# Cross-entropy with label smoothing: rows by blocks of 128, results turned on VectorE and stored in 128-byte pieces

## The chip, the cores and the metric

One core of one Trainium2 chip. The metric is device time in microseconds of one execution. The profile covers a little less: its span was about 1.8 us shorter than the time for the kernel before. Fast runs of one kernel in one set lay within 0.6% of their median (within 0.4% for the kernel before); the median of the same kernel differed by up to 0.6% between sets of runs (87.83 us in the first, 87.28 to 87.33 in the later ones), so kernels are compared only with the runs of the kernel before from the same set. A run over 1.5% above the fastest of the same kernel is called slow and left out of the ratios.

## The reference

```python
log_probs = logits - max(logits)                       # logits: 256 x 32000 f32
log_probs = log_probs - log(sum(exp(log_probs)))
smooth_targets = smoothing / 32000, plus 1 - smoothing at the label
return -sum(smooth_targets * log_probs, axis=-1)       # 256 f32
```

Per row the kernel needs the sum of exp(x), the sum of x and the logit at the label. 32.8 MB come in, 1 KB goes out.

## The kernel before

The 256 rows are two "blocks" of 128, one row per partition each. A block is streamed in tiles; each tile goes to VectorE (sum of x, L121) and to ScalarE (exp and its sum, L131). Large tiles share a ring of three buffers; the late, small tiles have buffers of their own. Tiles are named by their columns: the 6400 tile is the second of block 1. A transfer is "issued" when a queue sends it off, and it has "landed" when the last of its semaphore updates has come.

```python
WIDTHS = ((8000, 8000, 8000, 8000),
          (7872, 6400, 4736, 3584, 2752, 2176, 1728, 1472, 1280))
x = logits.rearrange("(p r) c -> p (r c)", r=R)        # partition p holds rows 2p, 2p+1
lab = small.tile([P, 2 * R], I32)                      # 128 pieces of 16 B, ScalarE's queue
...
for r in range(R):
    for t, w in enumerate(ws):
        xt = ring.tile(...) if w >= 6000 else tail.tile(...)
        nc.sync.dma_start(out=xt[:, :w], in_=x[:, col : col + w])   # SyncE's queue
        ...  # L121 on VectorE, L131 on ScalarE
    nc.scalar.activation(out=lse[:], in_=esum[:, n - 1 : n], func=AF.Ln, bias=se_pre[:])
    nc.vector.tensor_tensor(out=res[:, r : r + 1], in0=lse[:], in1=lin[:], op=ALU.add)
nc.sync.dma_start(out=out.rearrange("(p r) -> p r", r=R), in_=res[:])  # 128 pieces of 8 B
```

The softmax here doesn't subtract the row's maximum and nothing guards it: scores larger than these inputs give would overflow.

Of the kernel before, what the change touches and what calls it, by code (L numbers as in the profile page):

```python
# [7 lines left out]
FP32 = mybir.dt.float32  # L8
BF16 = mybir.dt.bfloat16
I32 = mybir.dt.int32  # L10
ALU = mybir.AluOpType
# [11 lines left out]
def _exp_ln_table(arch: str) -> int | None:  # L23
    try:
        tables = hw_specs.get_activation_tables(arch)
    except Exception:
        return None
    for i, (_, funcs) in enumerate(tables.items()):
        if {AF.Exp, AF.Ln, AF.Copy}.issubset(funcs):
            return i  # L30
    return None


@with_exitstack
def kernel(
    ctx: ExitStack,
    tc: tile.TileContext,
    logits: bass.AP,
    labels: bass.AP,
    smoothing: bass.AP,  # L40
    out: bass.AP,
):
    nc = tc.nc
    B, C = logits.shape
    P = nc.NUM_PARTITIONS
    R = B // P
    assert B == R * P and len(WIDTHS) == R
    assert all(sum(ws) == C for ws in WIDTHS)
    eps = float(smoothing)
    c_small = eps / float(C)  # L50
    c_big = 1.0 - eps

    ring = ctx.enter_context(tc.tile_pool(name="ring", bufs=3))
    tail = ctx.enter_context(tc.tile_pool(name="tail", bufs=1))
    junk = ctx.enter_context(tc.tile_pool(name="junk", bufs=1))
    small = ctx.enter_context(tc.tile_pool(name="small", bufs=1))

    tbl = _exp_ln_table(nc.m.arch)
    if tbl is not None:
        nc.scalar.add_instruction(  # L60
            mybir.InstLoadActFuncSet(
                name=nc.get_next_instruction_name(),
                act_func_set_id=tbl,
                ins=[],
                outs=[],
            )
        )


    x = logits.rearrange("(p r) c -> p (r c)", r=R)  # L70

    lab = small.tile([P, 2 * R], I32, name="lab", tag="lab")
    nc.scalar.dma_start(
        out=lab[:], in_=labels.bitcast(I32).rearrange("(p f) -> p f", p=P)
    )
    rowoff = small.tile([P, R], I32, name="rowoff", tag="rowoff")
    for r in range(R):
        nc.gpsimd.iota(  # L78
            out=rowoff[:, r : r + 1],
            pattern=[[0, 1]],  # L80
            base=r * C,
            channel_multiplier=R * C,
        )
    flat_idx = small.tile([P, R], I32, name="flat_idx", tag="flat_idx")
    nc.gpsimd.tensor_tensor(  # L85
        out=flat_idx[:],
        in0=rowoff[:],
        in1=lab[:].rearrange("p (r two) -> p r two", two=2)[:, :, 0:1],
        op=ALU.add,
    )  # L90
    gat = small.tile([P, R], FP32, name="gat", tag="gat")
    for r in range(R):
        nc.gpsimd.indirect_dma_start(  # L93
            out=gat[:, r : r + 1],
            out_offset=None,
            in_=logits[:],
            in_offset=bass.IndirectOffsetOnAxis(ap=flat_idx[:, r : r + 1], axis=1),
        )

    res = small.tile([P, R], FP32, name="res", tag="res")  # L100
    col = 0
    for r in range(R):
        ws = WIDTHS[r]
        n = len(ws)
        esum = small.tile([P, n], FP32, name=f"esum{r}", tag=f"esum{r}")
        xsum = small.tile([P, n], FP32, name=f"xsum{r}", tag=f"xsum{r}")
        se_pre = small.tile([P, 1], FP32, name=f"se_pre{r}", tag=f"se_pre{r}")
        sx_pre = small.tile([P, 1], FP32, name=f"sx_pre{r}", tag=f"sx_pre{r}")
        lin_pre = small.tile([P, 1], FP32, name=f"lin_pre{r}", tag=f"lin_pre{r}")
        lin = small.tile([P, 1], FP32, name=f"lin{r}", tag=f"lin{r}")  # L110
        lse = small.tile([P, 1], FP32, name=f"lse{r}", tag=f"lse{r}")
        for t, w in enumerate(ws):
            if w >= RING_MIN:
                xt = ring.tile([P, max(WIDTHS[0])], FP32, name="xt", tag="xt")
            else:
                xt = tail.tile([P, w], FP32, name=f"xl{t}", tag=f"xl{t}")
            nc.sync.dma_start(out=xt[:, :w], in_=x[:, col : col + w])  # L117
            col += w
            h = w // 2
            jd = junk.tile([P, max(WIDTHS[0]) // 2], FP32, name="jd", tag="jd")  # L120
            nc.vector.scalar_tensor_tensor(  # L121
                out=jd[:, :h],
                in0=xt[:, :h],
                scalar=1.0,
                in1=xt[:, h:w],
                op0=ALU.mult,
                op1=ALU.add,
                accum_out=xsum[:, t : t + 1],
            )
            ja = junk.tile([P, max(WIDTHS[0])], BF16, name="ja", tag="ja")  # L130
            nc.scalar.activation(  # L131
                out=ja[:, :w],
                in_=xt[:, :w],
                func=AF.Exp,
                accum_out=esum[:, t : t + 1],
            )
            if t == n - 2:

                nc.vector.tensor_reduce(  # L139
                    out=sx_pre[:], in_=xsum[:, : n - 1], axis=AX.X, op=ALU.add  # L140
                )
                nc.vector.tensor_scalar(  # L142
                    out=lin_pre[:],
                    in0=sx_pre[:],
                    scalar1=-c_small,
                    scalar2=None,
                    op0=ALU.mult,
                )
                nc.vector.scalar_tensor_tensor(  # L149
                    out=lin_pre[:],  # L150
                    in0=gat[:, r : r + 1],
                    scalar=-c_big,
                    in1=lin_pre[:],
                    op0=ALU.mult,
                    op1=ALU.add,
                )
                nc.vector.tensor_reduce(  # L157
                    out=se_pre[:], in_=esum[:, : n - 1], axis=AX.X, op=ALU.add
                )
        nc.vector.scalar_tensor_tensor(  # L160
            out=lin[:],
            in0=xsum[:, n - 1 : n],
            scalar=-c_small,
            in1=lin_pre[:],
            op0=ALU.mult,
            op1=ALU.add,
        )
        nc.scalar.activation(  # L168
            out=lse[:], in_=esum[:, n - 1 : n], func=AF.Ln, bias=se_pre[:]
        )  # L170
        nc.vector.tensor_tensor(  # L171
            out=res[:, r : r + 1], in0=lse[:], in1=lin[:], op=ALU.add
        )
    nc.sync.dma_start(out=out.rearrange("(p r) -> p r", r=R), in_=res[:])


# [33 lines left out]
```

## Time and profile before

| | kernel before |
|---|---|
| time, median | 87.76 us (87.5 to 87.98) |
| span of the profiled run | 85.7 us |
| logits, mean rate over the span | 382 GB/s |
| ScalarE busy | 69% |
| VectorE busy | 44% |
| last store, issue to landing | 2.9 us |

The shares of busy time mislead here: ScalarE is idle early and full late. The costliest groups of the page (busy us and mean ns of one, then the idle time just before and what ended it) say so:

```profile
L131 ACT ACTIVATE ja<-xt 128x8000 bf16<-128x8000 f32 (+2 forms) x6 | 39.8, 6630 | 21.5 <-DMA xt<-in_logits_dram 21.5
L131 ACT ACTIVATE ja<-xl 128x4736 bf16<-128x4736 f32 (+6 forms) x7 | 16.2, 2314 | 0.3
```

Before the six large tiles ScalarE waited 21.5 us for data, before the seven late ones 0.3 us. The loads set the pace first; at the end loads and ScalarE run in step, with no slack in either.

### The profile page before, as it was taken

The page shows a single profiled execution, that of the slowest core. Times are in us where ns is not written, and L with a number is a line of the kernel's source. Part 1 is how long each engine was busy: PE and PEld are TensorE (multiplying, and loading weights), DVE is VectorE, ACT ScalarE, POOL GpSimd, SP SyncE. Part 2 cuts the span into 40 slices and gives each one's busy share as a digit, 9 for nine tenths or more (in the row PEclk, how much of TensorE's full clock was granted, in tenths as well). Part 3 has the DMA queues.
Part 4 walks back from the last instruction along what each step waited for, and adds up shares of the span by engine and source line. Part 5 has one row for each costly group of instructions (what it writes and reads, how often), then busy time and mean ns, then how long its engine had stood idle before and what let it go on. Part 6 is the DMA issues. An engine that isn't in the chain of part 4 may idle for free.

```text
span 85.7 us, 167 instructions
## 1 busy us (share of the span) xinstructions
DVE 37.3 (44%) x38; ACT 59.1 (69%) x29; POOL 6.5 (8%) x9
## 2 busy tenths in 40 slices
DVE  0000009900495009920694029706909294566700
ACT  5000009992499709992599829996999999999900
POOL 1000008973000000000000000000000000000000
DMA  7699899997999989999899989989999999997000
GB/s 209 269 433 433 344 463 478 433 463 343 433 478 433 448 358 433 478 433 460 367 397 470 470 382 418 490 354 424 442 431 428 394 425 424 413 415 323 0 1 0
DMA packets 2224, 32.77 MB, mean 382 GB/s; under 512 B 560, under 2 KB 560, under 8 KB 944
## 3 DMA queue, kind: packets, MB, share of 16 engines
q1 hardware_dynamic: 2016, 32.77, 90.3%
q10 hardware_dynamic: 144, 0.00, 0.1%
q0 software_dynamic: 64, 0.00, 0.1%
HBM read 32.77 MB, written 0.00 MB: 382 GB/s over the span
## 4 chain that ended last, share of the span: by engine, by line
DMA 58%; ACT 34%; issue 2%; SPq 1%; DVE 0%; ACTq 0%
DMA xt<-in_logits_dram 58%; ACT ja L131 33%; SPq L117 1%; ACT lse L168 0%; DVE res L171 0%; ACTq L131 0%
## 5 line engine op out<-in xcount | busy, mean ns | idle before, releaser
L131 ACT ACTIVATE ja<-xt 128x8000 bf16<-128x8000 f32 (+2 forms) x6 | 39.8, 6630 | 21.5 <-DMA xt<-in_logits_dram 21.5
L121 DVE SCALAR_TENSOR_TENSOR jd<-xt 128x4000 f32<-128x4000 f32 (+2 forms) x6 | 25.1, 4175 | 31.0 <-DMA xt<-in_logits_dram 31.0
L131 ACT ACTIVATE ja<-xl 128x4736 bf16<-128x4736 f32 (+6 forms) x7 | 16.2, 2314 | 0.3
L121 DVE SCALAR_TENSOR_TENSOR jd<-xl 128x2368 f32<-128x2368 f32 (+6 forms) x7 | 10.3, 1476 | 7.7 <-DMA xl<-in_logits_dram 7.7
L85 POOL TENSOR_TENSOR flat_idx<-rowoff,lab 128x2 int32<-128x2 int32 x1 | 4.1, 4084 | 12.2 <-DMA lab<-in_labels_dram 12.2
L93 POOL DMA_INDIRECT gat<-in_logits_dram,flat_idx x2 | 2.1, 1028 | 0.6 <-issue 0.3
L171 DVE TENSOR_TENSOR res<-lse,lin 128x1 f32<-128x1 f32 x2 | 0.3, 160 | 3.5 <-ACT lse L168 3.5
L60 ACT ACT_TABLE_LOAD x1 | 1.3, 1283 | 0.7 <-PEq L191 0.7
L131 ACT ACTIVATION_READ_ACCUMULATOR ja<-xl 128x1 f32 x7 | 1.3, 186 | 0.0
L157 DVE TENSOR_REDUCE se_pre<-esum 128x1 f32<-128x3 f32 (+1 forms) x2 | 0.3, 158 | 2.1 <-ACT ja L131 2.1
L131 ACT ACTIVATION_READ_ACCUMULATOR ja<-xt 128x1 f32 x6 | 1.1, 186 | 0.0
L168 ACT ACTIVATE lse<-esum,se_pre 128x1 f32<-128x1 f32 x2 | 0.6, 294 | 0.1
L121 DVE DVE_READ_ACCUMULATOR jd<-xl 128x1 f32 x7 | 0.6, 82 | 0.0
L121 DVE DVE_READ_ACCUMULATOR jd<-xt 128x1 f32 x6 | 0.5, 82 | 0.0
L149 DVE SCALAR_TENSOR_TENSOR lin_pre<-gat,lin_pre 128x1 f32<-128x1 f32 x2 | 0.3, 159 | 0.1
L139 DVE TENSOR_REDUCE sx_pre<-xsum 128x1 f32<-128x3 f32 (+1 forms) x2 | 0.3, 158 | 0.1
L160 DVE SCALAR_TENSOR_TENSOR lin<-xsum,lin_pre 128x1 f32<-128x1 f32 x2 | 0.3, 158 | 0.1
L142 DVE TENSOR_SCALAR lin_pre<-sx_pre 128x1 f32<-128x1 f32 x2 | 0.3, 154 | 0.1
L78 POOL IOTA rowoff<- 128x1 int32 x2 | 0.2, 118 | 0.4 <-PEq L205 0.4
L191 POOL MEMSET const-uint8-127<- 128x1 uint8 x1 | 0.1, 118 | 0.0
L191 POOL MEMSET const-float32-0.0<- 128x1 f32 x1 | 0.1, 98 | 0.2 <-issue 0.2
L191 POOL MEMSET const-bfloat16-1.0<- 128x1 bf16 x1 | 0.1, 113 | 0.0
(1 smaller groups left out, 0.1 us busy)
## 6 DMA issues: line engine op xcount, KB each, us to landing
xt<-in_logits_dram SPq DMA_DIRECT2D x4, 4000.0 KB, 21.5
xt<-in_logits_dram SPq DMA_DIRECT2D x1, 3936.0 KB, 21.3
xt<-in_logits_dram SPq DMA_DIRECT2D x1, 3200.0 KB, 19.4
xl<-in_logits_dram SPq DMA_DIRECT2D x1, 2368.0 KB, 24.6
xl<-in_logits_dram SPq DMA_DIRECT2D x1, 1792.0 KB, 28.4
xl<-in_logits_dram SPq DMA_DIRECT2D x1, 1376.0 KB, 31.3
xl<-in_logits_dram SPq DMA_DIRECT2D x1, 1088.0 KB, 33.4
xl<-in_logits_dram SPq DMA_DIRECT2D x1, 864.0 KB, 35.0
```

Source lines behind the costliest of these rows:

```text
L60: nc.scalar.add_instruction(mybir.InstLoadActFuncSet(name=nc.get_next_instruction_name(), act_func_set_id=tbl, ins=[], outs=[],))
L85: nc.gpsimd.tensor_tensor(out=flat_idx[:], in0=rowoff[:], in1=lab[:].rearrange("p (r two) -> p r two", two=2)[:, :, 0:1], op=ALU.add,)
L93: nc.gpsimd.indirect_dma_start(out=gat[:, r : r + 1], out_offset=None, in_=logits[:], in_offset=bass.IndirectOffsetOnAxis(ap=flat_idx[:, r ...
L117: nc.sync.dma_start(out=xt[:, :w], in_=x[:, col : col + w])
L121: nc.vector.scalar_tensor_tensor(out=jd[:, :h], in0=xt[:, :h], scalar=1.0, in1=xt[:, h:w], op0=ALU.mult, op1=ALU.add, accum_out=xsum[:, t ...
L131: nc.scalar.activation(out=ja[:, :w], in_=xt[:, :w], func=AF.Exp, accum_out=esum[:, t : t + 1],)
L139: nc.vector.tensor_reduce(out=sx_pre[:], in_=xsum[:, : n - 1], axis=AX.X, op=ALU.add)
L142: nc.vector.tensor_scalar(out=lin_pre[:], in0=sx_pre[:], scalar1=-c_small, scalar2=None, op0=ALU.mult,)
L149: nc.vector.scalar_tensor_tensor(out=lin_pre[:], in0=gat[:, r : r + 1], scalar=-c_big, in1=lin_pre[:], op0=ALU.mult, op1=ALU.add,)
L157: nc.vector.tensor_reduce(out=se_pre[:], in_=esum[:, : n - 1], axis=AX.X, op=ALU.add)
L168: nc.scalar.activation(out=lse[:], in_=esum[:, n - 1 : n], func=AF.Ln, bias=se_pre[:])
L191: nc = _bacc.Bacc("TRN2", target_bir_lowering=False, num_devices=1)
```

## The change

Block r becomes rows 128r to 128r+127, so that a block's 128 results are one contiguous 512 B of the output. Each block's results, one column of a 128x32 tile, are turned by a 32x32 transpose per group of partitions; then partitions 0, 32, 64 and 96 hold 32 results each, and the store has four pieces of 128 B in place of 128 of 8 B. The diff, cut to its core:

```diff
-    x = logits.rearrange("(p r) c -> p (r c)", r=R)
-    lab = small.tile([P, 2 * R], I32, name="lab", tag="lab")
+    lab = small.tile([P, R, 2], I32, name="lab", tag="lab")
     nc.scalar.dma_start(
-        out=lab[:], in_=labels.bitcast(I32).rearrange("(p f) -> p f", p=P)
+        out=lab[:], in_=labels.bitcast(I32).rearrange("(r p two) -> p r two", r=R, two=2)
     )
 ...  # iota base and multiplier follow the rows
 ...  # SQ = 32; one 128x32 tile res[r] per block, set to 0 by GpSimd; col starts at 0 in each block
-            nc.sync.dma_start(out=xt[:, :w], in_=x[:, col : col + w])
+            nc.sync.dma_start(out=xt[:, :w], in_=logits[r * P : (r + 1) * P, col : col + w])
 ...  # inside the loop over blocks:
-            out=res[:, r : r + 1], in0=lse[:], in1=lin[:], op=ALU.add
-        )
-    nc.sync.dma_start(out=out.rearrange("(p r) -> p r", r=R), in_=res[:])
+            out=res[r][:, 0:1], in0=lse[:], in1=lin[:], op=ALU.add
+        )
+        rest = small.tile([P, SQ], FP32, name=f"rest{r}", tag=f"rest{r}")
+        nc.vector.transpose(out=rest[:], in_=res[r][:])
+        nc.sync.dma_start(
+            out=out[r * P : (r + 1) * P].rearrange("(g i) -> g i", i=SQ),
+            in_=rest[0:P:SQ, :],
+        )
```

More of the change, by code (lines that the diff above doesn't have):

```diff
@@ L80 @@
             pattern=[[0, 1]],
-            base=r * C,
-            channel_multiplier=R * C,
+            base=r * P * C,
+            channel_multiplier=C,
         )
@@ L87 @@
         in0=rowoff[:],
-        in1=lab[:].rearrange("p (r two) -> p r two", two=2)[:, :, 0:1],
+        in1=lab[:, :, 0:1],
         op=ALU.add,
@@ L98 @@
         )
-    res = small.tile([P, R], FP32, name="res", tag="res")
-    col = 0
+    SQ = 32
+    res = []
     for r in range(R):
+        t = small.tile([P, SQ], FP32, name=f"res{r}", tag=f"res{r}")
+        nc.gpsimd.memset(t[:], 0.0)
+        res.append(t)
+    for r in range(R):
+        col = 0
         ws = WIDTHS[r]
```

## The prediction

> **What bounds the kernel now.** I read the page's chain first, then the groups with their idle times, then the windows of DMA rate, then the timeline around 40 to 60 us, and last the tail.
>
> The chain that ended last:
>
> ```profile
> ## 4 chain that ended last, share of the span: by engine, by line
> DMA 58%; ACT 34%; issue 2%; SPq 1%; DVE 0%; ACTq 0%
> DMA xt<-in_logits_dram 58%; ACT ja L131 33%; SPq L117 1%; ACT lse L168 0%; DVE res L171 0%; ACTq L131 0%
> ```
>
> More than half of the span is the wait for logits, the rest mostly the exponential (L131). To see whether the loads ever pause, the windows (us, busy times, clock, DMA share, GB/s):
>
> ```profile
> 20.00:30.00 10.00, 4.33 (x2) 6.96 (x2) 0.00 (x0) 1.00 1.03 442
> 40.00:50.00 10.00, 4.65 (x4) 7.26 (x3) 0.00 (x0) 1.00 1.00 429
> 50.00:60.00 10.00, 5.68 (x3) 8.28 (x3) 0.00 (x0) 1.00 0.97 418
> 60.00:70.00 10.00, 6.20 (x5) 9.94 (x5) 0.00 (x0) 1.00 1.00 425
> 70.00:80.00 10.00, 5.99 (x14) 9.81 (x11) 0.00 (x0) 1.00 0.89 367
> ```
>
> They don't: from 12 to about 79 us the DMA engines are full at some 430 GB/s. From 60 us on ScalarE is full too. The shrinking widths have been tuned so that each late tile lands just as the exponential before it ends; the timeline shows this (start, length, engine, line; in brackets the idle time before):
>
> ```profile
> 50.92 6.76 ACT L131 ACTIVATE ja<-xt 128x7872 bf16<-128x7872 f32 x1 [2.00 <-DMA xt<-in_logits_dram]
> 58.58 5.54 ACT L131 ACTIVATE ja<-xt 128x6400 bf16<-128x6400 f32 x1 [0.81 <-DMA xt<-in_logits_dram]
> 64.24 2.63 DVE L121 SCALAR_TENSOR_TENSOR jd<-xl 128x2368 f32<-128x2368 f32 x1 [2.15 <-DMA xl<-in_logits_dram]
> 64.24 4.15 ACT L131 ACTIVATE ja<-xl 128x4736 bf16<-128x4736 f32 x1
> ...
> 78.39 1.43 ACT L131 ACTIVATE ja<-xl 128x1472 bf16<-128x1472 f32 x1
> 78.40 0.93 DVE L121 SCALAR_TENSOR_TENSOR jd<-xl 128x736 f32<-128x736 f32 x1 [0.74 <-DMA xl<-in_logits_dram]
> ```
>
> VectorE waits for the DMA and starts its tile in the same hundredths of a microsecond as ScalarE: data and ScalarE are ready together. So there is no slack in the loads after about 40 us: if they slip by d, the end slips by d, less a few hundredths. The tail:
>
> ```profile
> 81.34 0.29 ACT L168 ACTIVATE lse<-esum,se_pre 128x1 f32<-128x1 f32 x1
> 81.66 0.16 DVE L171 TENSOR_TENSOR res<-lse,lin 128x1 f32<-128x1 f32 x1 [0.63 <-ACT lse L168]
> 81.85 0.35 SPq L174 DMA_DIRECT2D out_dram<-res  x1
> ```
> ```profile
> out_dram<-res SPq DMA_DIRECT2D x1, 1.0 KB, 2.9
> ```
>
> The store is issued at 81.85, lands 2.9 us later (84.78), and 0.95 us of closing instructions bring the span to 85.7. The measured 87.5 to 88.0 is the span plus about 1.8 us.
>
> [...] the 1 KB store takes 2.9 us, though the last of its packets ended at about 82.9, so 1.9 us of it come after the data left; and the queue of SyncE stands still at its waits (23.3 us in all before the store of L174). [...] The old store has 128 packets of 8 B, the new one four of 128 B: [...] 32 times fewer. In the trace the semaphore updates of the old store's 16 engines come one after the other from 83.09 to 84.78, which looks like writes that queue up on one small stretch of memory. [...] No transpose is in this trace, so I price it by its neighbours. [...] Row starts go from 256,000 B to 128,000 B apart here; [...] the first ran at 430 GB/s, so I expect no change of rate.
>
> **The change, part by part.**
>
> Rows. Block r is now rows 128r to 128r+127 rather than every second row. Tile widths, sizes, packet lengths and the work on ScalarE and VectorE stay as they were: 0.
>
> Labels. Each partition's two labels now come from two places, so 256 pieces of 8 B instead of 128 of 16 B. The old label load took 12.3 us for 2 KB: its packets take turns with those of the first logits tile on every engine (both have 8 per engine, both landed at 13 us). With 16 per engine I expect it at about 22.5 us, with the second tile. That pushes flat_idx (4.1 us) and the two gathers (landed by 27.2) back by 9.5 us, to some 36.7. Their reader L149 ran at 36.90, and VectorE has nothing urgent until the next tile at 41.57. Hidden: 0. The two memsets on GpSimd lie in its 12.2 us idle: 0.
>
> First store. This is the part that I think matters most, and the diff doesn't show it. In the instruction order of the changed kernel, SyncE's queue holds: four loads of 8000, the load of 7872, the store of block 0, then the load of 6400 and all later ones. The store waits for the first transpose. Before, the 6400 load was issued at 39.13, as soon as ScalarE gave its buffer back, 11 us ahead of need. Now:
> - block 0's res starts at 48.95 and takes 0.16, so 49.11; transpose about 0.19 plus a 0.03 gap, so 49.33; store issued at 49.36, takes 0.35 on the queue, so 49.71; the 6400 load is issued at about 49.76.
> - Meanwhile the engines run out: the 7872 tile lands at 50.89, its last packets end between 49.7 and 50.4 on the 16 engines. First packets of the kernel's first load came 1.0 us after its issue (0.74 to 1.75), so the new ones start at about 50.8, and on a pipe that has to fill again.
> - Size of the hole: the first tile was issued at 0.74 and released ScalarE at 12.96; later tiles of that size come 9.54 us apart (12.96, 22.57, 32.15, 41.57). So a load on an empty pipe has 12.96 - 0.74 - 9.54 = 2.68 us over its streaming time. The 6400 tile streams in 9.54 x 0.8 = 7.63. Release at 49.76 + 2.68 + 7.63 = 60.07 instead of 58.52: 1.5 us late. The kernel's first load may have met start-up costs that don't return, and the spread of the engines is reset, so I take 1.4.
> - The loads behind it are issued about 0.45 us apart and their semaphore lanes are free soon enough (7872 landed at 50.89, the store of block 0 by about 52), so they follow without a second hole. All are 1.4 later, and so is the end: +1.4.
>
> Second transpose. It is on the tail's path: a VectorE instruction of one column takes 0.16, the 4000-column one of L121 4.33, so 1.04 ns a column; 32 columns make 0.19, with the hand-over 0.03: +0.22.
>
> Second store. Same 0.35 issue, then four packets on (I expect) four engines. The first engine of the old store reported 1.24 us after issue, the last 2.93. With no queue of small writes I expect 1.3 to 2.0, say 1.5: 2.93 - 1.5 = -1.4.
>
> Sum: +1.4 + 0.22 - 1.4 = +0.2. On 87.76 this makes 88.0.
>
> **The rivals.**
>
> The store in the queue is hidden anyway. For it: the engines still have 1 us of work when the load is issued at 49.76, and its tile is needed only at 58.5. Against: it is rate, not need, that sets the landing, and an engine idle for 1 us is never given back. The time would be 87.76 + 0.22 - 1.4 = 86.6, still within 2%.
>
> The small store costs its receipt whatever its shape. [...] Against: the spread of 1.7 us between the engines' updates. With no gain at all, 87.76 + 1.4 + 0.22 = 89.4, just inside 2%.
>
> The new row distance, or label packets that disturb two tiles rather than one, slow the loads. 1% of 78 us of loading is 0.8 us; nothing in the trace speaks for it but nothing excludes it. Together with the hole it would give 88.8 or more.
>
> The gathers come so late that VectorE stalls in order at L149. It would need 4.5 us more than I estimate before the tile at 41.57 is held up; then the buffer ring would slip too. Unlikely.
>
> **Range and chances.** The hole may be 0.9 to 1.7, the store's gain 0.6 to 1.6, the transpose is known to 0.1; the two large terms are independent and cancel. 8 times in 10 I expect 87.0 to 89.1. For faster by 2% (under 86.0) the hole would have to be absent and the store better than estimated: 0.05. For slower by 2% (over 89.5) the store would have to gain nothing, or the loads be slower: 0.08. Within 2%: 0.87.
>
> **What would show each step right or wrong.** The timeline should show SyncE's load of 6400 columns at about 49.8 instead of 39.1, right after an out store; the DMA row should dip in the slices near 51 us; ScalarE should wait some 2.2 us, not 0.81, before the 6400 tile, start it near 60.0 and then run without waits to the logarithm at about 82.8. The last transpose should take about 0.2, the last store land 1.3 to 2.0 after issue. The label load should land near 22 us and flat_idx start then, with no tile before 49 us moved. If the 6400 tile starts at 58.6 as before, the hole is wrong; if the last store still takes 2.9, the gain is; if the tiles before 49 us come at other than 9.5 us spacing, the row distance matters and I missed it.

The sum came to +0.2: +1.4 for the hole, +0.22 for the second transpose, -1.4 for the last store, all three estimated from the trace of the kernel before. That the new row distance changes no rate was the expectation from the 430 GB/s of the old one; experiment 4 tests it.

## The result, and the profile after

| | before | after |
|---|---|---|
| time, median of 4 | 87.83 us | 88.84 us |
| ratio, 95% interval | | 1.0116 (1.0079 to 1.0154) |
| same on another occasion, 11 and 5 runs | 87.30 us | 88.62 us, ratio 1.0146 (1.0123 to 1.0170) |

A ratio is the mean time of one kernel's fast runs over that of the other's of the same rounds, so not quite the ratio of the medians. The change costs 1.2 to 1.5%: within 2%, inside the predicted range, but +1.0 to +1.3 us where +0.2 was predicted.

SyncE's queue first, in the timeline of the kernel before and then of the changed one (start, time from the first to the end of the last of the group, line, count):

```profile
0.74 38.72 SPq L117 DMA_DIRECT2D xt<-in_logits_dram  x6
39.51 11.73 SPq L117 DMA_DIRECT2D xl<-in_logits_dram  x7
```
```profile
0.74 29.38 SPq L119 DMA_DIRECT2D xt<-in_logits_dram  x5
49.73 0.63 SPq L179 DMA_DIRECT2D out_dram<-rest  x1
50.45 0.34 SPq L119 DMA_DIRECT2D xt<-in_logits_dram  x1
50.85 3.53 SPq L119 DMA_DIRECT2D xl<-in_logits_dram  x7
```

Before, the sixth large load was out by 39.5 us and the late ones followed at once. After, five large loads were issued, then the queue stood until block 0's store, and the sixth large load went out at 50.45. The DMA engines' view of the same moment, in 2 us windows (busy times, clock, then DMA share and GB/s), before and after:

```profile
50.00:52.00 2.00, 1.08 (x1) 1.08 (x1) 0.00 (x0) 1.00 1.01 435
52.00:54.00 2.00, 2.00 (x1) 2.00 (x1) 0.00 (x0) 1.00 0.95 410
```
```profile
50.00:52.00 2.00, 0.82 (x1) 0.82 (x1) 0.00 (x0) 1.00 0.66 167
52.00:54.00 2.00, 2.00 (x1) 2.00 (x1) 0.00 (x0) 1.00 0.67 269
54.00:56.00 2.00, 1.45 (x2) 2.00 (x1) 0.00 (x0) 1.00 0.99 422
```

That is the hole: 167 and 269 GB/s where 435 and 410 stood. ScalarE sees it as a longer wait before the 6400 tile, and as nothing later, since everything behind is late by the same amount:

```profile
22.81 6.87 ACT L133 ACTIVATE ja<-xt 128x8000 bf16<-128x8000 f32 x1 [2.86 <-DMA xt<-in_logits_dram]
...
60.64 5.54 ACT L133 ACTIVATE ja<-xt 128x6400 bf16<-128x6400 f32 x1 [2.60 <-DMA xt<-in_logits_dram]
...
83.41 0.29 ACT L170 ACTIVATE lse<-esum,se_pre 128x1 f32<-128x1 f32 x1
83.79 0.16 DVE L173 TENSOR_TENSOR res<-lse,lin 128x1 f32<-128x1 f32 x1 [0.68 <-ACT lse L170]
83.99 0.21 DVE L178 STREAM_TRANSPOSE rest<-res 128x32 f32<-128x32 f32 x1
84.23 0.54 SPq L179 DMA_DIRECT2D out_dram<-rest  x1
```

The 6400 tile starts at 60.64 rather than 58.58. The second tile is late too, 22.81 rather than 22.57: a small drift before the hole. From the tile at 60.64 to the logarithm at 83.41 it is 22.77 us, before it was 22.76. By the trace's semaphore updates the last store lands at 85.80, 1.57 us after its issue.

Added up for the two profiled runs, the span went from 85.74 to 86.69, +0.95: drift +0.27, hole +1.79 (60.64 - 58.58 less the drift), from the logarithm's end to the last store's issue +0.31 (0.22 to 0.53), landing of the last store -1.36 (2.93 to 1.57), closing instructions -0.06.

### The profile page after: what moved, and what is told of

It is laid out like the page before. It is cut to its first block, busy times and chain, and to the rows that moved or that the text cites. A ratio compares the mean times of both kernels' runs of the same rounds, so it can differ in the third digit from the quotient of the medians.

```text
span 86.7 us, 172 instructions
## 1 busy us (share of the span) xinstructions
DVE 37.7 (44%) x40; ACT 59.1 (68%) x29; POOL 6.3 (7%) x11
## 4 chain that ended last, share of the span: by engine, by line
DMA 51%; ACT 34%; issue 10%; DVE 1%; SPq 1%; DVEq 0%; ACTq 0%
DMA xt<-in_logits_dram 51%; ACT ja L133 33%; SPq L179 1%; ACT lse L170 1%; DVE rest L178 1%; DVE res L173 0%; DVEq L173 0%; ACTq L133 0%; SPq L119 0%
## 5 line engine op out<-in xcount | busy, mean ns | idle before, releaser
L90 POOL DMA_INDIRECT gat<-in_logits_dram,flat_idx x2 | 5.6, 2798 | 0.9 <-POOL flat_idx L82 0.6
L82 POOL TENSOR_TENSOR flat_idx<-rowoff,lab 128x2 int32<-128x2 int32 x1 | 0.2, 193 | 21.5 <-DMA lab<-in_labels_dram 21.5
```

The lines of the kernel that those rows point to most:

```text
L90: nc.gpsimd.indirect_dma_start(out=gat[:, r : r + 1], out_offset=None, in_=logits[:], in_offset=bass.IndirectOffsetOnAxis(ap=flat_idx[:, r ...
```

## The experiments

Eleven runs. Times are medians with the ratio to the kernel before of the same rounds.

**1. The early store from the other queue.** Same store at the same moment, issued by ScalarE.

```diff
-        nc.sync.dma_start(
+        (nc.scalar if r < R - 1 else nc.sync).dma_start(
             out=out[r * P : (r + 1) * P].rearrange("(g i) -> g i", i=SQ),
```

> The changed kernel with block 0's store issued from ScalarE's queue instead of SyncE's; same store, same moment. Theory (the place in SyncE's queue holds back the load of 6400 columns): that load is issued at about 39.3 us again, ScalarE starts the 6400 tile at 58.8 to 58.9 instead of 60.64, and the time falls by 1.8 us from 88.84 to about 87.05, 0.8 below before. Rival (the store's own traffic, or anything else of the changed kernel, makes the hole): the 6400 tile still starts near 60.6 and the time stays near 88.8.

Measured 86.93 us against 87.28, ratio 0.9969 (0.9943 to 0.9995). The queue's order and the wait before the 6400 tile:

```profile
0.74 39.10 SPq L119 DMA_DIRECT2D xt<-in_logits_dram  x6
39.90 15.87 SPq L119 DMA_DIRECT2D xl<-in_logits_dram  x7
```
```profile
59.04 5.54 ACT L133 ACTIVATE ja<-xt 128x6400 bf16<-128x6400 f32 x1 [0.81 <-DMA xt<-in_logits_dram]
```

The wait is 0.81 us again, as in the kernel before: the hole is gone, and with it 1.5 to 1.8% of the time (0.997 against 1.012 and 1.015), 1.3 to 1.5 us. The place in SyncE's queue is the cause, not the store. The gain over the kernel before is 0.3 us rather than the expected 0.8. The time itself, 86.93, is what was expected (87.05), but the 0.8 was counted from the kernel before at 87.83, and in this set that ran at 87.28; beyond this, the 6400 tile came 0.15 to 0.25 later than expected. ScalarE's queue took 1.06 us to issue this store, but ScalarE had nothing to do then.

The other queue does not free every load. The store now lands at 55.42, 5.5 us after its issue, and SyncE's last load (1280 columns) goes out only then, at 55.44, because it waits for that store's semaphore, which it uses again (us in total, times, longest):

```profile
SPq L119 <- DMA out_dram<-rest: 3.7, 1, 3.7
```

Its tile is needed only at 80.4, so here this cost nothing.

**2. The kernel before with an early store.** Column 0 stored after block 0, column 1 at the end; no transpose, old rows.

```diff
-    nc.sync.dma_start(out=out.rearrange("(p r) -> p r", r=R), in_=res[:])
+        nc.sync.dma_start(
+            out=out.rearrange("(p r) -> p r", r=R)[:, r : r + 1], in_=res[:, r : r + 1]
+        )
```

> The kernel before with its one store split in two: column 0 stored by SyncE right after block 0, column 1 at the end; no transpose, old rows, old labels. Theory (hole from the queue order alone): the load of 6400 columns is issued at about 49.5, its tile starts 10.2 us later at about 59.7 instead of 58.58, and the time is 87.8 + 1.1 = 88.9; the last store still takes about 2.9 us. Rival (an early store costs nothing, the hole needs the turned store): 87.8.

Measured 91.46 us, ratio 1.0494 (1.0457 to 1.0531): 4.2 us lost, not 1.1. In the profiled run the 6400 tile is 3.8 us late.

```profile
49.80 0.38 SPq L117 DMA_DIRECT2D xt<-in_logits_dram  x1
```
```profile
62.38 5.54 ACT L131 ACTIVATE ja<-xt 128x6400 bf16<-128x6400 f32 x1 [4.40 <-DMA xt<-in_logits_dram]
```
```profile
52.00:54.00 2.00, 2.00 (x1) 2.00 (x1) 0.00 (x0) 1.00 0.10 26
```

The load was issued at 49.80, near the expected 49.5, but its tile came 12.58 us later; in the changed kernel it was 10.19. From 52 to 54 us the engines finished next to nothing. In the trace the first packets of the load start at 50.8 to 51.3 on 14 engines and take 2.9 to 4.2 us each, against 1.1 to 1.8 in the changed kernel and 0.95 in the kernel before; the updates of the early store, 128 pieces of 4 B, come as late as 52.6. So this load was held up on the engines too, and not only in the queue. Four pieces in the same place cost nothing of the kind, so the turned form pays twice.

The same early store from ScalarE's queue (the edit of experiment 1 on this kernel):

> The kernel with the split store (128 pieces of 4 B after block 0), the early store issued from ScalarE's queue. With the early store in SyncE's queue the 6400 tile came 12.6 us after the issue of its load rather than 10.2, its first packets taking 3.5 us or more. Theory A (loads queue behind the small writes in the same queue; the queue order costs 1.2 and the writes 2.4): on the other queue both go, 6400 tile at 58.6 to 59.1 (pieces between those of a load cost some tenths, as the labels do), ratio 1.00 to 1.006. Theory B (small writes hold up the engines whatever the queue): 6400 tile at 60 to 61.5.

Measured 88.69 us over the three fast runs (a fourth, 89.86, was slow), ratio 1.0148 (1.0114 to 1.0182), so neither: moving the store to the other queue takes away 3.5% of the 4.9%, and over 1% remains though no load stands behind the store in its own queue. The profiled run was the slow one, so its timeline is not used. Theory A fails as put: the other queue removes most of the loss, not all. Where exactly the rest is lost stays open.

**3. The label pieces alone.** The kernel before with labels as 256 pieces of 8 B.

```diff
-    lab = small.tile([P, 2 * R], I32, name="lab", tag="lab")
+    lab = small.tile([P, R, 4], I32, name="lab", tag="lab")
     nc.scalar.dma_start(
-        out=lab[:], in_=labels.bitcast(I32).rearrange("(p f) -> p f", p=P)
+        out=lab[:, :, 0:2],
+        in_=labels.bitcast(I32).rearrange("(p r two) -> p r two", r=R, two=2),
     )
 ...  # flat_idx reads lab[:, :, 0:1]
```

> The kernel before with the labels loaded as 256 pieces of 8 B instead of 128 of 16 B; nothing else. Theory (the drift of 0.24 us before the second tile in the changed kernel comes from the label pieces between the pieces of the second tile): labels land at about 22.5 us, the second tile starts at about 22.8 instead of 22.57, and the time is 88.0 to 88.1. Rival (the drift comes from the new row distance): second tile at 22.57, time 87.8.

Measured 87.81 us against 87.28, ratio 1.0055 (1.0024 to 1.0086), so 0.2 to 0.75 us. GpSimd's wait for the labels ends at 24.2 us:

```profile
POOL flat_idx L86 <- DMA lab<-in_labels_dram: 23.2, 1, 23.2
```

The second tile, on which the test was set, started at 22.63, nearer to the rival (22.57) than to the theory (22.8); but the third came at 32.52 (before: 32.15) and the 6400 tile at 59.05 (58.58). One pair of profiles can't carry a difference this small, since the first tile alone starts anywhere from 12.82 to 13.38. The distance from the first tile to the second is steadier: 9.60 to 9.63 us in the six profiles with 128 label pieces (the slow one left out), 9.73 to 9.94 in the five with 256. The 7872 tile, the last before the hole, started on average 0.33 us later in those five. So the drift is the labels'; here it is larger than in the changed kernel and spread over two tiles.

**4. The rows alone.** Logits by blocks of 128, all else as before; rows and labels no longer belong together, which is wrong.

```diff
-            nc.sync.dma_start(out=xt[:, :w], in_=x[:, col : col + w])
+            nc.sync.dma_start(out=xt[:, :w], in_=logits[r * P : (r + 1) * P, col : col + w])
 ...  # col starts at 0 in each block
```

> The kernel before with only the logits rows by blocks of 128; labels and the store stay as they were, so the result is wrong on purpose. Theory (labels make the drift, row distance costs nothing): second tile at 22.57, tiles 9.5 apart, time 87.8. Rival (row distance): second tile at 22.8, time 88.05 or more.

Measured 87.39 us, ratio 1.0022 (0.9991 to 1.0052); second tile at 22.48, 6400 tile at 58.55 against 58.58. The distance between rows costs nothing that these runs resolve.

**5. What the shape of a store does.** The changed kernel's last store made plain: block 1's column as it lies, 128 pieces of 4 B side by side in 512 B.

```diff
+        if r == R - 1:
+            nc.sync.dma_start(
+                out=out[r * P : (r + 1) * P].rearrange("(p f) -> p f", f=1),
+                in_=res[r][:, 0:1],
+            )
+            continue
 ...  # block 0's store: from ScalarE's queue, as in experiment 1
```

> The changed kernel, except that block 1's results are stored as they lie, 128 pieces of 4 B, without the second transpose; block 0 stays as changed, the hole included. Theory (the turned store gains 1.3 to 1.4 us in its landing): last store lands 2.8 to 2.9 us after issue, time 1.0 to 1.1 above the changed kernel, ratio to before about 1.024. Rival (landing depends on the moment or the block, not the shape): 1.6 us, ratio about 1.009.

The kernel that ran was built on that of experiment 1, so it has no hole, unlike what the text says. Without the hole the expectation is a ratio of about 1.01. Measured 91.96 us, ratio 1.0508 (1.0475 to 1.0542). Against experiment 1 (86.93) that is 5 us more, and the landing alone explains it (KB, then us from issue to landing):

```profile
out_dram<-res SPq DMA_DIRECT2D x1, 0.5 KB, 6.9
```

6.9 us, not 2.8: both theories were too low. In block order a plain store would be far worse than the old one.

The opposite: the kernel before, with its last store of 128 pieces of 8 B sent to a scratch tensor in which the pieces lie 4 KB apart (zeros to the output at the start, wrong).

```diff
-    nc.sync.dma_start(out=out.rearrange("(p r) -> p r", r=R), in_=res[:])
 ...  # zeros to the output
+    far = nc.dram_tensor("far", (P, 1024), FP32, kind="Internal").ap()
+    nc.sync.dma_start(out=far[:, 0:R], in_=res[:])
```

> The kernel before whose last store goes to a scratch tensor with the 128 pieces of 8 B 4 KB apart instead of side by side; zeros go to the output at the start, so the result is wrong on purpose. Theory A (pieces that share a small stretch of memory wait for one another): the far store lands 1.3 to 1.8 us after issue. Theory B (each small piece costs, wherever it goes): 2.8 to 3.0 us as before.

One run, 85.92 us; only its landing is used:

```profile
far<-res SPq DMA_DIRECT2D x1, 1.0 KB, 1.4
```

The same 128 pieces of 8 B land in 1.40 us rather than 2.93, and all 16 engines report within 0.2 us. So small pieces are not slow as such. This run alone leaves a rival, since the scratch tensor is also another piece of memory. Experiment 2 speaks against it: both of its stores went to the output, 128 pieces of 4 B whose starts lie 8 B apart, and landed in (min, median, max of the two)

```profile
DMA to landing us min/median/max: 2.8/3.0/3.2
```

against 6.9 for the same pieces 4 B apart. With 128 pieces each time, the landing followed the distance from start to start: 4 B 6.88 us, 8 B 2.79 to 3.24 (whether the piece is 4 or 8 B; the 3.24 beside loads), 4 KB 1.40. So the closer the pieces lay, the later the store landed; that they hold each other up is the author's reading of it. The turned store (1.57 us) has only four.

**6. The changed kernel again, for the same rounds as the next two.**

> The changed kernel once more, on the same chip as the two below, to have all three against one set of runs of the kernel before. Expected ratio 1.012 as first measured. In its time, 0.2 to 0.3 us should again lie outside the span of the profile (time less span 2.0 to 2.1, where the kernel before has 1.8).

Measured 88.62 against 87.30, ratio 1.0146; 6400 tile at 60.36; time less span 2.00 on average. The time outside the span is as expected, the ratio a little above the 1.012.

**7. The turned store without its two costs.** Old rows, old labels; block 0's transpose writes the even columns of one tile, block 1's the odd ones, and there is one store of 4 pieces of 256 B, at the end.

```diff
+    rest = small.tile([P, SQ, R], FP32, name="rest", tag="rest")
 ...  # res[r]: one 128x32 tile per block, set to 0 by GpSimd, as in the changed kernel
+        nc.vector.transpose(out=rest[:, :, r], in_=res[r][:])
-    nc.sync.dma_start(out=out.rearrange("(p r) -> p r", r=R), in_=res[:])
+    nc.sync.dma_start(
+        out=out.rearrange("(g i) -> g i", i=R * SQ),
+        in_=rest[0:P:SQ].rearrange("g i r -> g (i r)"),
+    )
```

> The kernel before with its rows, its 16 B labels and one store, but the results turned: block 0's transpose writes the even places and block 1's the odd places of 64 results per group of 32 partitions, and one store at the end sends 4 pieces of 256 B. No early store, so no hole; no label drift. Theory (the gain of the changed kernel is its last store alone, 2.9 to 1.6 us, less 0.3 for transpose and hand-overs): 6400 tile at 58.6, last store lands 1.5 to 1.7 us after issue, span 1.0 to 1.1 below before, time 0.8 to 1.1 below. Rival (pieces of 4 x 256 B land no sooner, or two transposes cost more than their span): time equal to before.

Measured 86.69 us, ratio 0.9925 (0.9903 to 0.9946). 6400 tile and tail:

```profile
58.47 5.54 ACT L137 ACTIVATE ja<-xt 128x6400 bf16<-128x6400 f32 x1 [0.81 <-DMA xt<-in_logits_dram]
...
81.81 0.21 DVE L180 STREAM_TRANSPOSE rest<-res 128x32 f32<-128x32 f32 x1
82.05 0.62 SPq L181 DMA_DIRECT2D out_dram<-rest  x1
```

No hole, and the store lands at 83.67, 1.62 us after its issue. The mean span fell by 0.8 us (85.57 to 84.73), the time by 0.6; 0.2 is again lost outside the span. Both fall short of what was expected (1.0 to 1.1 and 0.8 to 1.1). Still, it is faster than both kernels.

With the labels loaded as 4 pieces of 512 B and turned on VectorE at the start as well:

```diff
+    labw = small.tile([P, 32, 2 * R], I32, name="labw", tag="labw")
+    nc.gpsimd.memset(labw[:], 0)
     nc.scalar.dma_start(
-        out=lab[:], in_=labels.bitcast(I32).rearrange("(p f) -> p f", p=P)
+        out=labw[0:P:32].rearrange("g i f -> g (i f)"),
+        in_=labels.bitcast(I32).rearrange("(g f) -> g f", g=P // 32),
     )
+    lab = small.tile([P, R, 32], I32, name="lab", tag="lab")
+    for r in range(R):
+        nc.vector.transpose(out=lab[:, r, :], in_=labw[:, :, 2 * r])
 ...  # flat_idx reads lab[:, :, 0:1]
```

> The kernel above with the labels loaded the same way, as 4 pieces of 512 B that VectorE turns at the start. Theory (each small label piece between two pieces of logits costs 0.02 to 0.04 us of the engines' time, 8 per engine in the kernel before): label load lands by about 5 us, second and later tiles 0.2 to 0.3 us earlier than in the kernel above, time lower by that. Rival (label pieces cost nothing unless there are 16 per engine): same time as the kernel above.

The 0.02 to 0.04 us for a piece were an estimate; in the profiles compared in experiment 3, eight pieces more per engine went with 0.10 to 0.34 us more from the first tile to the second, so 0.01 to 0.04 each.

Measured 86.43 us, ratio 0.9905 (0.9882 to 0.9927), the fastest by median. The labels landed at 7.9 us rather than 5; the second tile started at 22.43 against 22.45, not 0.2 to 0.3 earlier, and the 6400 tile at 58.33. But the intervals of the two overlap, and the mean spans are 84.73 and 84.67: whether the old label pieces cost anything is not settled.

**8. The time outside the span.** Time less span averaged 1.79 us for the kernel before and 2.08 for the changed one. To see whether the transpose is the cause, one transpose of zeros was put into VectorE's idle first microseconds of the kernel before.

```diff
 ...  # tin and tout: tiles of 128x32
+    nc.gpsimd.memset(tin[:], 0.0)
 ...
+    nc.vector.transpose(out=tout[:], in_=tin[:])
```

> The kernel before with one transpose of zeros on VectorE in its idle first microseconds, nothing else. It asks where the 0.2 to 0.3 us come from that the changed kernel's time has outside the profile's span. Theory (a program that holds this instruction costs that much before its first instruction): time less span 2.0 to 2.1, span as before, ratio 1.002 to 1.003. Rival (something else of the changed kernel): time less span 1.8, ratio 1.000.

Measured 87.50 us, ratio 1.0006 (0.9977 to 1.0034), time less span 1.92: about half of the effect. All kernels that turn results late have 1.94 to 2.08, but the one that turns labels as well has 1.82, which the theory does not allow. The cause is open.

## Why the prediction was right or wrong

The time lay in the range and in the predicted class, and the main mechanism was the right one. The sum, though, came out at +0.2 where +1.0 and +1.3 were measured. Step by step:

- **No slack in the loads.** Right: the hole moved the end by its full size, with 22.77 us from the 6400 tile to the logarithm against 22.76.
- **First store, order in the queue.** Right; experiments 1 and 7 remove it by the queue alone and by having no early store. The size, +1.4, was +1.79. The 6400 load was issued at 50.45 rather than 49.76: 0.28 of that is the drift, 0.28 is the store's issue, which took 0.63 where the prediction used the old store's 0.35, and the rest is hand-overs and 0.02 of transpose. From issue to tile it took 10.19, against 10.31 worked out from the kernel's first load, so cutting 1.5 to 1.4 was right: the whole shortfall of 0.4 is the later issue less the drift.
- **Labels.** This is the step that was wrong in kind: "Hidden: 0". The prediction followed the labels to their reader, and that was right (landed at 22.6, the gathers at 36.9, their reader at 37.09 just not held up). It did not ask what the 256 pieces do to the loads that they are interleaved with. Alone they cost 0.55% (experiment 3); in the profiled pair the tiles before the hole slipped by 0.27 us.
- **Second transpose.** +0.22 was +0.31: 0.21 for the instruction (expected 0.19), and res waited 0.09 us after the logarithm rather than 0.03.
- **Second store.** -1.4 was -1.36, and the reason given, writes that queue up on one small stretch of memory, passed its test (2.93 us side by side, 1.40 at 4 KB), with the number that decides being the distance between pieces (experiment 5).
- **Not foreseen:** 0.2 to 0.3 us outside the span, cause open.

So the term for the hole was too small by 0.4, the labels missing by 0.3, the transpose short by 0.1, and 0.2 to 0.3 lay where the profile does not look. All errors point the same way; only the width of the range took them up. Of the rivals, "hidden anyway" and "the receipt costs the same whatever its shape" both fell, and so did the row distance (experiment 4: ratio 1.0022, 0.9991 to 1.0052); label pieces that disturb the loads, which the prediction named beside the row distance and then priced at nothing, were real. That this rival's figure, 88.8 or more, hits the measured 88.84 is luck: it holds 0.8 for them where 0.3 was seen, and nothing for the larger hole.

## What to carry to other kernels

What was measured here, as things to look at elsewhere. The store that was moved into the loop took a place in its queue, and the loads behind it waited for the store's data: the 6400 load was issued at 50.45 us rather than 39.13, and sending the store from another queue took 1.3 to 1.5 us off the time. So try another queue or the end before judging what else such a store does, and look there too for loads that wait for its semaphore (3.7 us in experiment 1). Turning the results into four long pieces brought the landing from 2.93 to 1.57 us, and the number that decided was how close the small pieces lay in memory, and not their count alone: 128 pieces landed in 1.40 to 6.88 us (experiment 5). When a small transfer shares the engines with a saturated stream, count its pieces as a possible cost to the stream, even if nobody waits for it: 256 label pieces in place of 128 cost 0.55% here (experiment 3).

## What these runs measured of small stores

- The landing, from issue: 128 pieces of 8 B 4 KB apart 1.40 us, the same side by side 2.93, 128 of 4 B 8 B apart 2.79 and 3.24, the same side by side 6.88, 4 of 128 B 1.57, 4 of 256 B 1.62.
- The load behind a store of 128 pieces of 4 B was held up: its first packets on 14 engines took 2.9 to 4.2 us, behind 4 pieces of 128 B 1.1 to 1.8, with no store ahead 0.95 (experiment 2).
- In the profile of the changed kernel each store of four pieces shows 5 semaphore updates, where the store of the kernel before shows 16; the first of the five comes 0.55 us ahead of the others (50.73 and 51.28 to 51.34, 85.17 and 85.72 to 85.79).
- The issue of a store of four pieces took 0.54 to 0.63 us on SyncE and 1.06 on ScalarE. For a store of 128 pieces it took 0.33 to 0.35 on SyncE, and 0.35 on ScalarE in the slow profile of experiment 2. Why is not shown.
